# A hybrid encoder layer in split float32: the high halves of streamed weight chunks are asked for one chunk further ahead than the low halves

## The chip, the cores and the metric

The kernel runs on one core of a Trainium2 chip. The metric is device time in microseconds (us), the median of several runs. The kernel before takes 702.0 us, the median of 3 runs (702.0, 702.2, 700.14).

## The reference

One layer, sequence 512, model width 1024, one batch, everything float32. `h` is the RMS-normed input, and its projection `z = h @ w_in` feeds two groups of heads; then an output projection, a SwiGLU block and a gated embedding follow:

```
h = rms_norm(x, g_mix); z = h @ w_in
c_q, c_kv, k_r, hq, hf_f, hf_b, hi, hg = split(z)
a = mla(c_q, c_kv, k_r, ...)         # 4 heads of latent attention, dense softmax
r = hgrn2(hq, hf_f, hf_b, hi, hg, ...)   # 4 heads, gated linear recurrence, both directions
x = x + concat(a, r) @ w_o
h = rms_norm(x, g_ffn); x = x + (silu(h @ w_gate) * (h @ w_up)) @ w_down
gate = sigmoid(rms_norm(x, g_ple) @ w_ple_gate); x = x + gate * (p @ w_ple_proj)
```

The part up to and including `w_o` is called the mixer here, the SwiGLU block the FFN.

## The kernel before

Activations lie transposed, model width on the 128 partitions and the 512 tokens along a row. Each float32 operand of a large product is split into a rounded high part and a low remainder, and a product is three matmuls (`mm3`, lines 141 to 144): high by high (L142), low by high (L143), high by low (L144). Transposes, the recurrence and the sums of squares use plain float32 matmuls.

The mixer streams its weights in 30 chunks of 128x1024 floats (512 KB): 12 for the recurrence's queries and forget gates (`w_hf`), 4 for its values (`w_i`), 4 for its output gates, 4 for the attention's half of `w_o` (`w_oa`), 2 for `w_pp`, 4 for the other half of `w_o` (`w_or`). A chunk has a high tile (`whi`) and a low tile (`wlo`). `weights` (line 148) fills them. The first two chunks are loaded by SyncE as raw float32 and split by ScalarE and VectorE. For the other 28, GpSimd's queue starts a DMA that casts while it loads, which gives the high part (L155); ScalarE writes its negative into the low tile (L156); and a second GpSimd DMA of the same 512 KB adds the source to it (L157), which leaves the remainder. So each chunk is read twice, and its second read waits for a ScalarE copy, which waits for the first.

`wnext` hands out the chunks in order and keeps `AHEAD = 3` of them requested. `wpool` has 4 buffers of each kind (`WB`), 3 of the raw kind, so the high tile of a chunk goes where that of the chunk 4 before it was, once TensorE is done with that.

All other tiles of 128x512 come from a queue of slots of 2 KB a partition: `SLOTS = 74` slots, given out first in, first out. When the mixer ends, `wpool` is closed, and 22 slots (`SLOTS2`) in its place join the queue; the FFN takes its weights (`halves`, L1024, and `pair_seven`, L1102), its sums and its activations from it, so the number of slots says how far its loads can run ahead.

TensorE's work in the mixer is two streams merged: the dense one (products of the streamed chunks, tiles `wi`, `wt`, `wo`, `pp`) and the latency-bound one (attention and recurrence: tiles `s` scores, `p` softmax, `pT` transposed softmax, `av` values, `pd`, `px`, `pk`, `po`). The latency stream has 5 PSUM banks, given out in turn: a bank that held scores `s` becomes free when ScalarE has made `p` of them (L557). The order on each engine is then set by a scheduler, which plays a timeline while the kernel is built; so an edit of one request moves instructions on all engines.

Of the kernel before, what the change touches and what calls it, by code (L numbers as in the profile page):

```python
# [9 lines left out]
F32R = mybir.dt.float32r  # L10
# [5 lines left out]
P = 128  # L16
# [4 lines left out]
EPS = 1e-6  # L21
QK_SCALE = 192 ** -0.5
FPARTS = (4, 4, 4, 4, 3, 3)
SLOTS = 74
SLOTS2 = 22
DAHEAD = 2

# [1 line left out]
AHEAD = 3  # L29
WB = 4  # L30
# [4 lines left out]
LO_DVE = 2  # L35
# [82 lines left out]
def layer_kernel(ctx: ExitStack, tc: tile.TileContext, io, out):  # L118
    nc = tc.nc
    act, dve, pool, pe, sp = nc.scalar, nc.vector, nc.gpsimd, nc.tensor, nc.sync  # L120
# [6 lines left out]
    wpool = mixer.enter_context(tc.tile_pool(name="wpool", bufs=WB))  # L127
    A = Slots(spool, SLOTS, "u")
    B = Slots(ppool, 8, "b")


    def split(hi, lo, src, scale=None, eng=dve):

        if scale is None:
            act.activation(hi, src, AF.Copy)  # L135
            eng.tensor_tensor(lo, src, hi, ALU.subtract)  # L136
        else:
            act.activation(hi, src, AF.Copy, scale=scale)
            dve.scalar_tensor_tensor(lo, src, scale, hi, ALU.mult, ALU.subtract)
# [5 lines left out]

    nw = [0]

    def weights(src, cols, by_dma=False):


        nw[0] += 1
        hi = wpool.tile([P, 1024], F32R, tag="whi", name=f"whi{nw[0]}")
        lo = wpool.tile([P, 1024], F32R, tag="wlo", name=f"wlo{nw[0]}")
        if by_dma:
            pool.dma_start(hi[:, :cols], src)  # L155
            act.activation(lo[:, :cols], hi[:, :cols].bitcast(F32), AF.Copy, scale=-1.0)  # L156
            pool.dma_start(lo[:, :cols], src, accum_op=ALU.add)  # L157
        else:
            raw = wpool.tile([P, 1024], F32, tag="raw", bufs=RAWB, name=f"raw{nw[0]}")
            sp.dma_start(raw[:, :cols], src)  # L160
            split(hi[:, :cols], lo[:, :cols], raw[:, :cols])
        return hi, lo
# [126 lines left out]
    def load_k(k):  # L289

        if k:
            sp.dma_start(xT[k], io["xT"][k])
        raw = wpool.tile([P, 1024], F32, tag="raw", bufs=RAWB, name=f"rawl{k}")
        hi = wpool.tile([P, 1024], F32R, tag="whi", name=f"whil{k}")
        lo = wpool.tile([P, 1024], F32R, tag="wlo", name=f"wlol{k}")
        sp.dma_start(raw[:, :256], io["w_q"][:, k * 256 : k * 256 + 256])
        if k == 0:
            sp.dma_start(vec, io["vec"])
        if k == 1:
            sp.dma_start(pos, io["pos"])  # L300
            sp.dma_start(cst[:, C_FREQ:], io["cst"][:, C_FREQ:])
        sp.dma_start(raw[:, 256:576], io["w_kv"][:, k * 320 : k * 320 + 320])
        for c in (slice(0, 256), slice(256, 576)) if k == 0 else (slice(0, 576),):
            split(hi[:, c], lo[:, c], raw[:, c])
            if c.start == 0:
                split(hT[k][0], hT[k][1], xT[k], vec[:, V_MIX + k : V_MIX + k + 1])
        ws.append((hi, lo))
# [10 lines left out]
    for k in range(KT):  # L318
        load_k(k)
        query_k(k)  # L320
        if k == 1:
            rotary_tables()
        squares(sq, xT[k], k == 0)
        if k < KT - 2:
            key_k(k)
# [271 lines left out]

    wlist = deque()
    ahead = deque()
    nd = [0]  # L600

    def wnext():
        while wlist and len(ahead) < AHEAD:
            nd[0] += 1
            ahead.append(weights(*wlist.popleft(), by_dma=nd[0] > LO_DVE))
        return ahead.popleft()

    def w_in_tile(d):

        w = wnext()  # L610
        o = BD.get("wi")
        for k in range(KT):
            mm3(o, cut(w, k * P, k * P + P), hT[k], k == 0, k == KT - 1)
            if k % 2:
                yield 1.3
        z = A.get("z")
        dve.tensor_tensor(z, o, bc1, ALU.mult)
        BD.put(o)
        d.append(z)

    def w_in_tokens(evacuate):

        for half in range(2):
            ws = [wnext(), wnext()]
            for jp in range(2):
                o = [BD.get("wt0"), BD.get("wt1")]
                for c in range(2):
                    for k in range(4 * c, 4 * c + 4):
                        a = (k % 4) * 256
                        for i in range(2):  # L630
                            j = 2 * jp + i
                            mm3(o[i][:, :256], cut(hT[k], j * P, j * P + P), cut(ws[c], a, a + 256), k == 0, k == KT - 1)
                        if k % 2:
                            yield 1.3
                for i in range(2):
                    evacuate(2 * jp + i, slice(half * 256, half * 256 + 256), o[i][:, :256])
                BD.put(*o)
# [242 lines left out]
    def w_o_half(half, src, banks):  # L880

        for c in range(2):
            ws = [wnext() for _ in range(2)] if half else None
            os_ = []
            for m in range(4 * c, 4 * c + 4):
                if not half and m % 2 == 0:
                    w = wnext()
                o = banks.get("wo")
                os_.append(o)
                if half:  # L890
                    continue
                for k in range(4):
                    a = ((m % 2) * 4 + k) * P
                    mm3(o, cut(w, a, a + P), src[k], k == 0, k == 3)
                dve.tensor_tensor(xT[m], xT[m], o, ALU.add)
                banks.put(o)
                yield 2.6
            if half:

                ki = [(k, i) for k in range(4) for i in range(4)]  # L900
                for k, i in ki if c == 0 else sorted(ki, key=lambda x: x[1]):
                    a = ((i % 2) * 4 + k) * P
                    mm3(os_[i], cut(ws[i // 2], a, a + P), src[k], k == 0, k == 3)
                for i in range(4):
                    residual(4 * c + i, os_[i], V_FFN, sq2, h2)
                banks.put(*os_)
# [283 lines left out]
    f = 0  # L1190
# [136 lines left out]
```

## Time and profile before

| what | value |
|---|---|
| median of 3 runs | 702.0 us |
| the profiled execution | 700.41 us |
| its span on the core | 698.6 us |
| TensorE (matmul) busy | 686.4 us, 98% |
| VectorE busy | 509.5 us, 73% |
| ScalarE busy | 383.2 us, 55% |
| GpSimd busy | 111.1 us, 16% |
| read from HBM | 88.33 MB, 129 GB/s over the span |

The profiled execution took 700.41 us, of which the span on the core is 698.6 us; the remaining 1.8 us lie around it. TensorE was at its full granted clock all the way. Engines are PE (TensorE), PEld (its weight loads), DVE (VectorE), ACT (ScalarE), POOL (GpSimd), SP (SyncE); a q behind a name means its sequencer. An arrow `<-` behind an idle time names what ended it.

### The profile page before, as it was taken

Reading aid. Unit: us, or ns where it says so; the run is one execution under the profiler, and the core shown is the slowest. Engines: PE = TensorE matmul, PEld = TensorE weight load, DVE = VectorE, ACT = ScalarE, POOL = GpSimd, SP = SyncE. Lnnn points to the kernel's source line nnn. Section 1 sums busy time; section 2 is a strip of 40 time slices with the busy share of each in tenths; the row PEclk is TensorE's granted clock in tenths of the full one; section 3 lists DMA queues with packets and bytes.
Section 4 is the critical chain, followed back from the end, with each engine's and each line's share of the span. In section 5 each row is a group of like instructions: output and inputs, shape, how many; then the busy total and the mean of one; then the engine's idle time right before and its main releaser. Section 6 shows DMA issues by size and latency. Waiting matters only on the chain.

```text
span 698.6 us, 11350 instructions
## 1 busy us (share of the span) xinstructions
PE 686.4 (98%) x4170; PEld 604.2 (86%) x4170; DVE 509.5 (73%) x1031; ACT 383.2 (55%) x808; POOL 111.1 (16%) x144
## 2 busy tenths in 40 slices
PE   9999999899999999999989999999999999999997
PEld 8888887699878888878788999999999999998886
DVE  6944489797987943679987977877677578768663
ACT  7857795686645645535544554445544545546421
POOL 6233421101212222010111100001100110100000
PEclk9999999999999999999999999999999999999999
DMA  7575555543657657322456456345655664563111
GB/s 241 164 171 136 124 145 97 119 86 84 157 123 208 156 138 189 90 66 61 147 129 163 115 145 178 92 115 145 166 130 130 158 138 123 123 179 112 55 60 61
DMA packets 44264, 91.18 MB, mean 131 GB/s; under 512 B 5424, under 2 KB 11568, under 8 KB 44208
## 3 DMA queue, kind: packets, MB, share of 16 engines
q0 software_dynamic: 14976, 41.43, 28.8%
q1 hardware_dynamic: 29232, 49.02, 22.3%
q8 instruction: 33, 0.54, 0.3%
q14 instruction: 23, 0.19, 0.1%
HBM read 88.33 MB, written 2.10 MB: 129 GB/s over the span
## 4 chain that ended last, share of the span: by engine, by line
PE 86%; issue 8%; DMA 2%; ACT 2%; POOL 1%; DVE 1%; SPq 0%; POOLq 0%; ACTq 0%
PE p L144 8%; PE p L143 8%; PE p L142 8%; PE dn L143 5%; PE dn L144 5%; PE dn L142 5%; PE wi L143 4%; PE wi L142 4%; PE wi L144 4%; PE pg L144 2%; PE pg L142 2%; PE pg L143 2%; PE wo L142 2%; PE wo L144 2%; PE wo L143 2%
## 5 line engine op out<-in xcount | busy, mean ns | idle before, releaser
L142 PE MATMUL p<-bh,whi 128*128 128x256 f32 x432 | 122.3, 284 | 2.4 <-ACT whi L135 2.3
L143 PE MATMUL p<-bl,whi 128*128 128x256 f32 x432 | 121.8, 283 | 0.0
L144 PE MATMUL p<-bh,wlo 128*128 128x256 f32 x432 | 121.3, 283 | 0.0
L142 PEld LDWEIGHTS p<-bh,whi 128*128 128x128 f32 x432 | 82.7, 192 | 3.3 <-ACT whi L135 3.2
L143 PEld LDWEIGHTS p<-bl,whi 128*128 128x128 f32 x432 | 82.8, 192 | 0.1
L144 PEld LDWEIGHTS p<-bh,wlo 128*128 128x128 f32 x432 | 82.5, 192 | 0.1
L143 PE MATMUL dn<-al,whi 128*128 128x512 f32 x176 | 68.7, 390 | 0.0
L144 PE MATMUL dn<-ah,wlo 128*128 128x512 f32 x176 | 68.5, 389 | 0.0
L142 PE MATMUL dn<-ah,whi 128*128 128x512 f32 x176 | 67.7, 390 | 0.0
L1170 POOL DMA_DIRECT2D wlo<-in_w_d x32 | 27.4, 877 | 202.4 <-ACT wlo L1169 160.5
L1112 DVE TENSOR_TENSOR S<-A,A 128x512 f32<-128x512 f32 x36 | 24.4, 689 | 40.0 <-DMA A<-in_w_up 19.5
L135 ACT ACTIVATE whi<-A 128x512 fp32r<-128x512 f32 x54 | 33.6, 626 | 35.0 <-DMA A<-in_w_gate 22.8
L142 PE MATMUL wi<-hh,whi 128*128 128x512 f32 x128 | 51.2, 400 | 0.0
L144 PE MATMUL wi<-hh,wlo 128*128 128x512 f32 x128 | 50.9, 397 | 0.0
L143 PE MATMUL wi<-hl,whi 128*128 128x512 f32 x128 | 50.5, 394 | 0.0
L135 ACT ACTIVATE whi<-S 128x512 fp32r<-128x512 f32 x72 | 42.6, 623 | 10.3 <-DVE S L1112 9.0
L156 ACT ACTIVATE wlo<-whi 128x1024 fp32r<-128x1024 f32 x28 | 29.7, 1060 | 33.4 <-DMA whi<-in_w_hf 12.0
L136 DVE TENSOR_TENSOR wlo<-S,whi 128x512 fp32r<-128x512 f32 x72 | 46.3, 681 | 1.0 <-ACT whi L135 1.0
L135 ACT ACTIVATE whi<-raw 128x512 fp32r<-128x512 f32 (+2 forms) x42 | 25.5, 625 | 31.6 <-DMA raw<-in_w_up 9.7
L136 DVE TENSOR_TENSOR wlo<-A,whi 128x512 fp32r<-128x512 f32 x54 | 36.8, 682 | 3.1 <-ACT whi L135 3.1
L144 PEld LDWEIGHTS dn<-ah,wlo 128*128 128x128 f32 x176 | 33.1, 188 | 6.9
L142 PEld LDWEIGHTS dn<-ah,whi 128*128 128x128 f32 x176 | 33.0, 188 | 6.4
(342 smaller groups left out, 1840.6 us busy)
## 6 DMA issues: line engine op xcount, KB each, us to landing
A<-in_w_gate SPq DMA_DIRECT2D x36, 256.0 KB, 4.4
A<-in_w_up SPq DMA_DIRECT2D x36, 256.0 KB, 3.8
wlo<-in_w_d POOLq DMA_DIRECT2D x32, 256.0 KB, 5.3
whi<-in_w_hf POOLq DMA_DIRECT2D x14, 512.0 KB, 4.6
wlo<-in_w_hf POOLq DMA_DIRECT2D x14, 512.0 KB, 5.7
raw<-in_w_d SPq DMA_DIRECT2D x24, 256.0 KB, 2.8
x<-in_xT SPq DMA_DIRECT2D x16, 256.0 KB, 4.4
raw<-in_w_pg SPq DMA_DIRECT2D x16, 256.0 KB, 3.5
```

Of the source, the lines that this page charges most:

```text
L135: act.activation(hi, src, AF.Copy)
L136: eng.tensor_tensor(lo, src, hi, ALU.subtract)
L142: pe.matmul(o, lhsT=l[0], rhs=r[0], start=start, stop=False)
L143: pe.matmul(o, lhsT=l[0], rhs=r[1], start=False, stop=False)
L144: pe.matmul(o, lhsT=l[1], rhs=r[0], start=False, stop=stop)
L156: act.activation(lo[:, :cols], hi[:, :cols].bitcast(F32), AF.Copy, scale=-1.0)
L1112: dve.tensor_tensor(r[n], r[a], r[b], op)
L1170: pool.dma_start(lo[:, n], src, accum_op=ALU.add)
```

## The change

`weights` is cut in two. `high` takes a high tile and starts its casting DMA; `weights` gets that tile and does the rest (ScalarE's copy and the adding DMA). `wnext` asks for the high part of one chunk more before it asks for the low part of the oldest chunk that has none. High tiles get 5 buffers, which is 4 KB a partition more, and `SLOTS` falls from 74 to 72, which is 4 KB less.

```diff
-SLOTS = 74
+SLOTS = 72
...
-    def weights(src, cols, by_dma=False):
+    def high(src, cols):
...
+        hi = wpool.tile([P, 1024], F32R, tag="whi", bufs=WB + 1, name=f"whi{nw[0]}")
+        pool.dma_start(hi[:, :cols], src)
+        return hi
+
+    def weights(src, cols, hi=None):
...
+        by_dma = hi is not None
+        if not by_dma:
+            nw[0] += 1
+            hi = wpool.tile([P, 1024], F32R, tag="whi", bufs=WB + 1, name=f"whi{nw[0]}")
         lo = wpool.tile([P, 1024], F32R, tag="wlo", name=f"wlo{nw[0]}")
         if by_dma:
-            pool.dma_start(hi[:, :cols], src)
             act.activation(lo[:, :cols], hi[:, :cols].bitcast(F32), AF.Copy, scale=-1.0)
             pool.dma_start(lo[:, :cols], src, accum_op=ALU.add)
...
     def wnext():
-        while wlist and len(ahead) < AHEAD:
+        while wlist and len(ahead) + len(highs) <= AHEAD:
+            c = wlist.popleft()
             nd[0] += 1
-            ahead.append(weights(*wlist.popleft(), by_dma=nd[0] > LO_DVE))
+            highs.append((*c, high(*c)) if nd[0] > LO_DVE else c)
+            if len(highs) > 1 or nd[0] <= LO_DVE:
+                ahead.append(weights(*highs.popleft()))
+        if len(ahead) < AHEAD and highs:
+            ahead.append(weights(*highs.popleft()))
         return ahead.popleft()
```

Line numbers behind the first function shift by 8, behind `wnext` by 15. The numbers at the ends of tile names also shift by a few.

On GpSimd's queue, around the value chunks (`in_w_i`), the order before is high part, low part of the same chunk, high part of the next:

```order
L155 DMA whi_1511<-in_w_i 128x1024
L157 DMA wlo_1512<-in_w_i 128x1024
L155 DMA whi_1624<-in_w_i 128x1024
L157 DMA wlo_1625<-in_w_i 128x1024
L155 DMA whi_1705<-in_w_i 128x1024
```

In the changed kernel the low part of a chunk stands behind the high part of the next one (`wlo_1515` belongs to `whi_1436`, `wlo_1628` to `whi_1513`):

```order
L152 DMA whi_1513<-in_w_i 128x1024
L165 DMA wlo_1515<-in_w_i 128x1024
L152 DMA whi_1626<-in_w_i 128x1024
L165 DMA wlo_1628<-in_w_i 128x1024
L152 DMA whi_1707<-in_w_i 128x1024
```

Each high part has moved up by one low part on this queue; the number of DMAs is the same.

On ScalarE, during the softmax of the second attention head, the order before has the copy of chunk 14 (`wlo_1625`) directly ahead of the last exponential, `p_1404`:

```order
L557 ACTIVATE p_1364,mx<-s_1356,mx 128x512
L557 ACTIVATE p_1384,mx<-s_1376,mx 128x512
L156 ACTIVATE wlo_1625<-whi_1624 128x1024
L557 ACTIVATE p_1404,mx<-s_1396,mx 128x512
L135 ACTIVATE pTh_1423<-pT_1418 128x512
```

In the changed kernel that chunk's copy (`wlo_1628` of `whi_1513`) stands four exponentials earlier, and the copy near `p_1406` is that of the next chunk and behind it:

```order
L164 ACTIVATE wlo_1628<-whi_1513 128x1024
L565 ACTIVATE p_1318,mx<-s_1310,mx 128x512
L565 ACTIVATE p_1337,mx<-s_1329,mx 128x512
L700 ACTIVATE z_795<-z_795 128x512
L700 ACTIVATE t_1468<-t_1468 128x512
L565 ACTIVATE p_1366,mx<-s_1358,mx 128x512
L565 ACTIVATE p_1386,mx<-s_1378,mx 128x512
L135 ACTIVATE pTh_1425<-pT_1420 128x512
L751 ACTIVATE dm<-dm 128x24 x2
L565 ACTIVATE p_1406,mx<-s_1398,mx 128x512
L164 ACTIVATE wlo_1709<-whi_1626 128x1024
```

The copies have moved from ahead of the softmax they stood in to places further from it.

On SyncE's queue, at the start of the FFN's second part, the order before asks for the last plain weights (`raw`) and then for the four blocks of the first pair of `pair_seven` (`A_507` to `A_510`):

```order
L1024 DMA raw_3709<-in_w_gate 128x512
L1024 DMA raw_3742<-in_w_up 128x512
L1024 DMA raw_3748<-in_w_up 128x512
L1102 DMA A_507_3811<-in_w_gate 128x512
L1102 DMA A_509_3815<-in_w_up 128x512
L1102 DMA A_508_3813<-in_w_up 128x512
L1102 DMA A_538_3997<-in_w_gate 128x512
L1102 DMA A_510_3817<-in_w_gate 128x512
```

The changed kernel asks for them in a similar order, out of 72 + 22 slots:

```order
L1039 DMA raw_3703<-in_w_gate 128x512
L1039 DMA raw_3709<-in_w_gate 128x512
L1117 DMA A_509_3815<-in_w_up 128x512
L1039 DMA raw_3742<-in_w_up 128x512
L1117 DMA A_510_3817<-in_w_gate 128x512
L1117 DMA A_507_3811<-in_w_gate 128x512
L1117 DMA A_508_3813<-in_w_up 128x512
L1117 DMA A_538_3997<-in_w_gate 128x512
```

The same loads stand there; `A_509` has moved ahead of the last plain weight.

## Rows read from the trace of the kernel before

**Rows 1.** The page, share of the span by engine: busy us (share), number of instructions.
```profile
PE 686.4 (98%) x4170; PEld 604.2 (86%) x4170; DVE 509.5 (73%) x1031; ACT 383.2 (55%) x808; POOL 111.1 (16%) x144
```

**Rows 2.** Busy us by stretch: length, then each engine (instructions), clock, DMA share, GB/s.
```profile
100.00:120.00 20.00, 20.00 (x92) 16.50 (x91) 18.94 (x50) 14.15 (x29) 4.30 (x5) 1.00 0.48 106
120.00:140.00 20.00, 17.48 (x90) 13.17 (x89) 15.34 (x39) 11.55 (x24) 3.68 (x5) 1.00 0.53 113
...
340.00:360.00 20.00, 17.36 (x108) 14.72 (x109) 18.21 (x33) 11.24 (x21) 3.38 (x5) 1.00 0.60 159
```

**Rows 3.** Timeline of PE, 124 to 130 us: start, duration, instruction [idle before <- releaser].
```profile
126.42 0.39 PE L144 MATMUL wi<-hh,wlo 128*128 128x512 f32 x1
126.66 0.39 PE L142 MATMUL wi<-hh,whi 128*128 128x512 f32 x1
129.40 0.55 PE L571 MATMUL pT<-cst,p 128*128 128x128 f32 x3 [2.35 <-ACT p L557]
```

**Rows 4.** Timeline of ACT, 122 to 130 us.
```profile
124.99 0.19 ACT L557 ACTIVATION_READ_ACCUMULATOR p<-s,mx 128x1 f32 x1
127.62 1.06 ACT L156 ACTIVATE wlo<-whi 128x1024 fp32r<-128x1024 f32 x1 [2.44 <-issue]
128.58 0.67 ACT L557 ACTIVATE p<-s,mx 128x512 f32<-128x512 f32 x1
```

**Rows 5.** Timeline of POOL, 108 to 132 us.
```profile
110.58 0.55 POOL L155 DMA_DIRECT2D whi<-in_w_i  x1 [2.22 <-PE wi L144]
119.74 0.85 POOL L157 DMA_DIRECT2D wlo<-in_w_i  x1 [8.61 <-ACT wlo L156]
120.29 1.13 POOL L155 DMA_DIRECT2D whi<-in_w_i  x1
```

**Rows 6.** DMA issues of 118 to 131 us, KB each, us from issue to landing.
```profile
wlo<-in_w_i POOLq DMA_DIRECT2D x2, 512.0 KB, 5.4
whi<-in_w_i POOLq DMA_DIRECT2D x1, 512.0 KB, 7.3
```

**Rows 7.** DMA issues of 0 to 118 us.
```profile
whi<-in_w_i POOLq DMA_DIRECT2D x1, 512.0 KB, 3.9
```

**Rows 8.** Waits of 0 to 345 us, ScalarE's copies L156: us in total, times, longest.
```profile
ACT wlo L156 <- DMA whi<-in_w_hf: 12.0, 7, 6.8
...
ACT wlo L156 <- DMA whi<-in_w_oa: 7.8, 3, 3.6
...
ACT wlo L156 <- DMA whi<-in_w_pp: 3.8, 1, 3.8
...
ACT wlo L156 <- DMA whi<-in_w_or: 3.7, 3, 2.4
```

**Rows 9.** Timeline of PE, 122 to 131 us: a step from wi to transposes and back.
```profile
123.73 0.40 PE L144 MATMUL wi<-hh,wlo 128*128 128x512 f32 x1
123.97 0.63 PE L571 MATMUL pT<-cst,p 128*128 128x128 f32 x4
124.35 0.48 PE L142 MATMUL wi<-hh,whi 128*128 128x512 f32 x1
124.67 0.40 PE L143 MATMUL wi<-hl,whi 128*128 128x512 f32 x1
```

**Rows 10.** First use of the value chunks by PE, of the rows of tile wlo.
```profile
L143 PE MATMUL wt<-wlo,hh x64: 277/283/365, 141.4 to 184.0; 128*128 128x256 f32 x64
```

**Rows 11.** Timeline of PE, 336 to 358 us.
```profile
350.04 0.39 PE L142 MATMUL p<-bh,whi 128*128 128x256 f32 x1 [1.11 <-ACT whi L135]
...
355.45 0.39 PE L142 MATMUL p<-bh,whi 128*128 128x256 f32 x1 [1.24 <-ACT whi L135]
```

**Rows 12.** Busy us by stretch, as rows 2, of 345 to 355 us.
```profile
345.00:350.00 5.00, 3.93 (x18) 2.82 (x17) 4.12 (x7) 3.06 (x6) 1.91 (x3) 1.00 0.84 244
350.00:355.00 5.00, 4.14 (x28) 3.52 (x28) 4.09 (x8) 1.78 (x4) 0.37 (x1) 1.00 0.99 242
```

**Rows 13.** SyncE's queue, 285 to 360 us: what its loads waited for.
```profile
SPq L1024 <- DVE t L1079: 14.1, 1, 14.1
SPq L1024 <- PE wo L144: 10.9, 2, 10.7
SPq L1024 <- PE ff L143: 10.8, 1, 10.8
```

**Rows 14.** DMA issues of 340 to 356 us.
```profile
A<-in_w_up SPq DMA_DIRECT2D x4, 256.0 KB, 4.8
```

More of the change, by code (lines that the diff above doesn't have):

```diff
@@ L146, in layer_kernel @@
     nw = [0]
-    def weights(src, cols, by_dma=False):
+    def high(src, cols):
         nw[0] += 1
-        hi = wpool.tile([P, 1024], F32R, tag="whi", name=f"whi{nw[0]}")
+        hi = wpool.tile([P, 1024], F32R, tag="whi", bufs=WB + 1, name=f"whi{nw[0]}")
[6 more added lines that the diff above has]
+            hi = wpool.tile([P, 1024], F32R, tag="whi", bufs=WB + 1, name=f"whi{nw[0]}")
         lo = wpool.tile([P, 1024], F32R, tag="wlo", name=f"wlo{nw[0]}")
         if by_dma:
-            pool.dma_start(hi[:, :cols], src)
             act.activation(lo[:, :cols], hi[:, :cols].bitcast(F32), AF.Copy, scale=-1.0)
@@ L293, in load_k @@
         raw = wpool.tile([P, 1024], F32, tag="raw", bufs=RAWB, name=f"rawl{k}")
-        hi = wpool.tile([P, 1024], F32R, tag="whi", name=f"whil{k}")
+        hi = wpool.tile([P, 1024], F32R, tag="whi", bufs=WB + 1, name=f"whil{k}")
         lo = wpool.tile([P, 1024], F32R, tag="wlo", name=f"wlol{k}")
@@ L599, in layer_kernel @@
     ahead = deque()
+    highs = deque()
     nd = [0]
     def wnext():
-        while wlist and len(ahead) < AHEAD:
+        while wlist and len(ahead) + len(highs) <= AHEAD:
+            c = wlist.popleft()
             nd[0] += 1
-            ahead.append(weights(*wlist.popleft(), by_dma=nd[0] > LO_DVE))
+            highs.append((*c, high(*c)) if nd[0] > LO_DVE else c)
[3 more added lines that the diff above has]
+            ahead.append(weights(*highs.popleft()))
         return ahead.popleft()
```

## The prediction

> **What bounds the kernel now.** I read the page's busy shares first: TensorE is busy 686.4 of 698.6 us, 98%, the next engine 73% [rows 1]. So whatever the change does to other engines counts only where TensorE stands still, and all its idle time is 12.2 us, start and end included. The second view is the busy time in stretches of 20 us. Two stretches inside the kernel fall visibly short: 120 to 140 us, with 17.48 us busy, and 340 to 360 us, with 17.36; the stretch before the first is full [rows 2]. The first lies in the mixer, where the change works, the second in the first part of the FFN, where only the two slots it takes away reach. The granted clock is 1.00 in both, so these are waits.
>
> The third view is the timeline of 120 to 131 us on three engines, to be read backwards. TensorE starts a `wi` matmul at 126.66 and the next instruction, a transpose `pT`, at 129.40; it waited 2.35 us for ScalarE's exponential `p` [rows 3]. At the ordinary step of 0.24 us (126.42 to 126.66, same rows) the hole costs 2.74 - 0.24 = 2.5 us. All four inputs of that transpose had served earlier transposes, so what it waits for must be the PSUM bank that the late exponential still reads. ScalarE had finished the exponential before it at about 125.2, then stood still for 2.44 us, made the low-part copy L156 of a weight chunk at 127.62, and only then the exponential, at 128.58 [rows 4]. Its queue runs in order, so the exponential waited behind the copy, and the copy for its chunk's high part. The profile names the releaser "issue"; the DMA view shows the cause: that high part took 7.3 us from issue to landing [rows 6], and 120.29 + 7.3 = 127.6 is when the copy starts. GpSimd had issued it 0.55 us after the adding DMA of the chunk ahead [rows 5]; an earlier one of the same size, `in_w_i` in an uncrowded stretch, landed after 3.9 us [rows 7]. So the mixer's one hole is a high part asked for too late and behind another transfer.
>
> **The change, part by part.** *Requests moved.* 28 casting and 28 adding DMAs stay 28 and 28, ScalarE keeps its 28 copies, TensorE its matmuls. Each high part is issued ahead of the low part of the chunk before. Its buffer is that of the chunk five before, so the request does not wait longer than the low part it now precedes, which waits for the chunk four before its own, the same chunk. GpSimd is blocked no more than before: it waits for what it would have waited for one instruction later.
>
> *The hole at 126.66.* The copy of that chunk now stands four exponentials earlier on ScalarE, its data asked for a whole chunk earlier; the copy near the critical exponential stands behind it. I take the whole 2.5 us off, less 0.1 for what any reordering leaves: **-2.4 us**. Bounds: 0 if another wait takes the place, -2.5 at most.
>
> *ScalarE's other waits for high parts.* 12.0 + 7.8 + 3.8 + 3.7 = 27.3 us [rows 8]. TensorE's two stretches show that, apart from the one hole, they were hidden behind dense matmuls; I cost their going at 0. The cover is the dense stream, and it stays.
>
> *Order of TensorE.* Written out, the old order changes 137 times between plain float32 products (transposes, recurrence) and split ones, the new one 121 times: 8 visits fewer. A visit costs a little: the matmul after four transposes takes 0.32 us to the next (124.35 to 124.67) against 0.24 otherwise [rows 9], so some 0.1 us with its entry. 8 x 0.1 = **-0.8 us**; bounds 0 and -1.5.
>
> *The low parts.* Each now stands behind a high part on the same software queue. From the rows, following another transfer cost 7.3 - 3.9 = 3.4 us [rows 6, 7]. Cover: the low part of the first value chunk was issued at 119.74 and landed 5.4 us later, at 125.1 [rows 5, 6]; its first use is at 141.4 [rows 10], 16 us on. I cost it at 0. The Trainium skill ("DMA: Bandwidth & Descriptors", section "Queues, rings and completion order") says that each DMA engine consumes descriptors in ring order; it speaks against this change, as it makes every low part the later of two. The trace agrees with it in the one pair above, 7.3 us for the follower; by it the sum is the same as long as the 16 us stand.
>
> *Two slots fewer, 94 instead of 96 in the FFN.* There loads do wait for slots: 14.1, 10.9 and 10.8 us in single waits [rows 13]. When slots come free, the transfers bunch: a DMA share of 0.84 and 0.99 in 345 to 355 us [rows 12], and TensorE waits 1.11 and 1.24 us for splits of these weights [rows 11]. No row shows the price of a slot. From below: 0, if the slots in question are free anyway. From above: a slot carries a 256 KB load that takes 4.8 us there [rows 14], so two loads that each fall in line behind a released slot add at most 2 x 4.8 = 9.6 us. SyncE's order is nearly the old one, so I take 0, nearest to the end at which the same events release the same loads, and keep the upper end for the range.
>
> *The start.* One high part is now issued ahead of the first `rs_tok` on GpSimd; such an issue takes 0.55 to 1.13 us [rows 5], and TensorE has dense work of several us there: 0.
>
> **Sum.** -2.4 - 0.8 = -3.2 us against the profiled execution's 700.4: 697.2 us. That execution lies 1.6 us below the median of the runs shown (702.0), and half of that, 0.8, is added for a median: **698.0 us**. A measurement of this kernel can tell about 0.3%, 2.1 us, from no change; -3.2 is just beyond it.
>
> **The rivals.**
>
> *A new hole for the old one (no change).* All engines' orders are drawn anew by the scheduler. ScalarE's copies, which used to come when their data had landed, now tend to wait for the low buffer, that is for TensorE to finish the chunk four before. If a copy stands ahead of an exponential or of a `kT` of the recurrence and TensorE still has one piece of that chunk ahead of it, say 12 matmuls of 0.24 us, 2.9 us, it costs about what the old hole did. For it: ScalarE's queue is in order, and the old hole was of this kind. Against it: one such hole in the 28 copies before. Time: 698.0 + 2.9 = 700.9 us.
>
> *The FFN starved by two slots (slower).* The stage of 340 to 360 us is the one place where TensorE waits for loads. If one load falls in line, +4.8; if both do, +9.6, against -3.2 elsewhere. Midway, 698.0 + 7.2 = 705.2 us. It decides from 3.2 + 2.1 = 5.3 us of added waiting in that stretch. For it: the DMA share of 0.99 and the long slot waits. Against it: one in 48 slots is little, and the long waits are for events (sums of blocks, finished products) that a slot more or less does not move.
>
> *The low parts come late (no change).* If followers land 3.4 us late, the rule of the ring order would show as TensorE waiting at a chunk's first high-by-low matmul (L144). Once it would cost 3.4 us: 698.0 + 3.4 = 701.4. The cover of 16 us speaks against it, the 7.3 us of the one follower for it. The page named above has the rule that gives it.
>
> *The change does not do what it says.* Excluded by the order: each high part does stand one low part earlier on GpSimd's queue.
>
> **How the numbers follow.** Forecast, the hole gone and nothing of size new: 0.50. New hole: 0.25. Late low parts: 0.05. FFN starved: 0.20. Within the forecast case a gain of 3.2 with its bounds of 0 to 4 us falls short of 2.1 about one time in seven, 0.07; the starved FFN ends slower by over 0.3% in 0.15 and within in 0.05; the new hole goes faster in 0.05, slower in 0.03, same in the rest. Faster 0.50 - 0.07 + 0.05 = 0.48; slower 0.15 + 0.03 = 0.18; same 0.34. The range: the forecast's own is 698.0 less 2 (a smaller FFN wait, since some FFN splits now come before the mixer's end) and plus 1.5; the no-change cases reach to 701.4; what lies above is most of the starved case. 695.5 to 703.0 leaves out 0.15 above and about 0.05 below.
>
> **What would show it.** Right: TensorE idle for `p` L557 under 0.5 us in 120 to 140; ScalarE's waits of L156 for high parts down from 27.3 us to under 8; adding DMAs landing later than 5.4 us after their issue, with no wait of TensorE at L144 in the mixer; the stretch of 340 to 360 us near its 17.4 us busy; everything after it earlier by about 3 us. Wrong: a hole of over 2 us at another place in 30 to 300 us, then the first rival; a busy time under 14 us in 340 to 360, then the second; waits at L144 for a DMA of `wlo`, then the third. A span within 1 us of 698.6 with the hole gone would mean that the gain was given back in the FFN, and the sum lacked that term.

## The result and the profile after

The changed kernel takes **693.7 us** (median; 693.2 to 694.6), the kernel before 701.7 us beside it: a ratio of 0.9873, interval 0.984 to 0.9906. The gain is 8.0 us, and 693.7 lies below the range that the forecast gave. Of the two profiled executions, the one after takes 693.5 us with a span of 691.7, against 700.4 and 698.6: 6.9 us are to be found in the traces.

The page after, the line that answers to [rows 1]: TensorE has lost 3.8 us of busy time and 3.1 us of idle time, ScalarE is 3.3 us busier.

```profile
PE 682.6 (99%) x4170; PEld 604.6 (87%) x4170; DVE 510.3 (74%) x1031; ACT 386.5 (56%) x808; POOL 108.7 (16%) x144
```

Busy time by stretch, after (columns as in [rows 2]). Both stretches that fell short before are full, 17.48 and 17.36 us then, 20.00 now. In exchange TensorE falls short in 320 to 340 us, 18.27 us busy against 19.86 before, while VectorE (the third engine of the row) has no hole there in either kernel:

```profile
120.00:140.00 20.00, 20.00 (x113) 16.81 (x112) 17.42 (x48) 13.63 (x28) 2.04 (x4) 1.00 0.49 101
...
320.00:340.00 20.00, 18.27 (x78) 13.82 (x77) 20.00 (x41) 10.29 (x18) 0.00 (x0) 1.00 0.17 52
340.00:360.00 20.00, 20.00 (x146) 18.89 (x145) 18.98 (x33) 12.34 (x24) 3.44 (x5) 1.00 0.66 187
```

TensorE's waits after (total, times, longest). The transpose that waited 2.35 us for the exponential [rows 3] is not among them, and a product has to wait for a late low part, once:

```profile
PE wo L142 <- ACT ppo L967: 0.9, 1, 0.9
PE ff L142 <- ACT whi L135: 0.9, 1, 0.9
PE wi L144 <- DMA wlo<-in_w_hf: 0.7, 1, 0.7
PE dn L142 <- ACT ah L135: 0.5, 1, 0.5
```

ScalarE's copies (now L164) waited 27.3 us for high parts [rows 8]; they wait 3.4 us for them now, and else for TensorE to give back a low buffer:

```profile
ACT wlo L164 <- PE wi L144: 5.7, 5, 2.2
ACT wlo L164 <- PE wt L143: 4.0, 3, 2.6
ACT wlo L164 <- DMA whi<-in_w_hf: 3.4, 1, 3.4
```

And the requests of 118 to 131 us (KB each, us to landing), 7.3 and 5.4 us before [rows 6]:

```profile
whi<-in_w_i POOLq DMA_DIRECT2D x2, 512.0 KB, 3.8
wlo<-in_w_i POOLq DMA_DIRECT2D x2, 512.0 KB, 6.1
```

**Where the time went.** Three places in the two timelines cut the span: the first residual sum of the output projection's last half (VectorE), the first FFN product `ff`, and the last product `p` (TensorE). Two more lines stand with them: the end of the last head (`rTl`) and the first step of the block sums (`xa`), both on VectorE. Before:

```profile
286.72 0.69 DVE L136 TENSOR_TENSOR rTl<-r,rTh 128x512 fp32r<-128x512 f32 x1 [3.14 <-ACT rTh L135]
...
289.95 2.48 DVE L999 TENSOR_TENSOR x<-x,wo 128x512 f32<-128x512 f32 x4 [1.09 <-PE wo L144]
...
295.19 0.39 PE L142 MATMUL ff<-hh,whi 128*128 128x512 f32 x1
...
316.61 0.74 DVE L1077 SCALAR_TENSOR_TENSOR xa<-x,vec,rsbc 128x512 f32<-128x512 f32 x1
...
625.79 0.28 PE L144 MATMUL p<-bh,wlo 128*128 128x256 f32 x1
```

After:

```profile
276.31 0.68 DVE L136 TENSOR_TENSOR rTl<-r,rTh 128x512 fp32r<-128x512 f32 x1
...
281.19 2.48 DVE L1014 TENSOR_TENSOR x<-x,wo 128x512 f32<-128x512 f32 x4 [4.20 <-PE wo L144]
...
291.87 0.39 PE L142 MATMUL ff<-hh,whi 128*128 128x512 f32 x1
...
311.43 0.74 DVE L1092 SCALAR_TENSOR_TENSOR xa<-x,vec,rsbc 128x512 f32<-128x512 f32 x1
...
618.91 0.28 PE L144 MATMUL p<-bh,wlo 128*128 128x256 f32 x1
```

By the first `ff` the changed kernel is 3.3 us ahead, about what the forecast summed. From the first `ff` to the last `p`, a stage whose code the change does not touch, it takes 327.0 us instead of 330.6 and gains 3.6 more. Everything behind keeps its length. Of the 3.6 us, 1.8 are waits of TensorE, 3.5 us in the stage before and 1.7 after; the other 1.8 are steps between products that are 0.1 to 0.2 us longer than usual, of which the kernel before has more, mostly in the first 20 us of the stage and around 345 to 355 us. I call that stretch the **FFN stage**, and the time from the first residual sum to the first `ff` the **lead** of the residuals: 5.2 us before, 10.7 after.

### The profile page after: what moved, and what is told of

It reads as the page before. It is cut to its first block, busy times and chain, and to the rows that moved or that the text cites. A ratio compares the mean times of both kernels' runs of the same rounds, so it can differ in the third digit from the quotient of the medians.

```text
span 691.7 us, 11366 instructions
## 1 busy us (share of the span) xinstructions
PE 682.6 (99%) x4170; PEld 604.6 (87%) x4170; DVE 510.3 (74%) x1031; ACT 386.5 (56%) x808; POOL 108.7 (16%) x144
## 4 chain that ended last, share of the span: by engine, by line
PE 88%; DVE 5%; DMA 4%; issue 1%; ACT 1%; SPq 1%; ACTq 0%; DVEq 0%
PE p L144 9%; PE p L143 9%; PE p L142 9%; PE dn L143 6%; PE dn L144 6%; PE dn L142 6%; PE wi L144 4%; PE wi L143 4%; PE wi L142 4%; PE pg L144 2%; PE pg L143 2%; PE pg L142 2%; PE wo L144 2%; PE wo L142 2%; PE wo L143 2%; PE po L852 1%
## 5 line engine op out<-in xcount | busy, mean ns | idle before, releaser
L144 PE MATMUL p<-bh,wlo 128*128 128x256 f32 x432 | 122.2, 283 | 0.0
L144 PEld LDWEIGHTS p<-bh,wlo 128*128 128x128 f32 x432 | 82.9, 192 | 0.2 <-DVE wlo L136 0.2
L144 PE MATMUL dn<-ah,wlo 128*128 128x512 f32 x176 | 68.5, 389 | 0.0
L144 PE MATMUL wi<-hh,wlo 128*128 128x512 f32 x128 | 50.6, 395 | 0.7 <-DMA wlo<-in_w_hf 0.7
L144 PEld LDWEIGHTS dn<-ah,wlo 128*128 128x128 f32 x176 | 33.0, 188 | 7.0
L136 DVE TENSOR_TENSOR wlo<-raw,whi 128x512 fp32r<-128x512 f32 (+2 forms) x42 | 28.5, 687 | 14.5 <-ACT whi L135 14.3
L164 ACT ACTIVATE wlo<-whi 128x1024 fp32r<-128x1024 f32 x28 | 29.8, 1063 | 16.2 <-PE wi L144 5.7
```

The source lines that it names most:

```text
L144: pe.matmul(o, lhsT=l[1], rhs=r[0], start=False, stop=stop)
```

## The experiments

One table first; what each run was for follows. Stage and lead are read as above from one profiled execution each; the mixer is the time from the first `wi` product to the first `ff`; times are medians, with the interval of the ratio to the kernel before. One execution is a rough measure. Two of one order (the kernel before and e4_ahead4) differ by 0.8 us in the stage and 0.3 in the mixer. Six kernels (the changed one, e2_slots2_24, e5_slots2_20, x1_hold, r1_after, r2_after) share TensorE's order from the first `wi` for 228 us; that stretch took from 227.8 to 229.8 us, mostly because a low part near 41 us came 0 to 1.4 us late. And some stages hold a time at the lower clock (last section): it took 3.4 us each from x3_six, x1_hold, e1_slots72 and y1_l96, 1.7 from x2_l104 and another 1.7 from its mixer. The whole time of the kernel before lay between 697.8 and 706.2 us in 25 executions of one session.

| kernel | high buffers | slots in the FFN | mixer us | lead us | FFN stage us | time us (ratio) |
|---|---|---|---|---|---|---|
| before | 4 | 96 | 263.1 | 5.2 | 330.6 | 701.7 |
| e4_ahead4 | 4 | 96 | 263.4 | 5.2 | 329.9 | 700.6 (0.9952 to 1.0001) |
| x5_raw2 | 5 | 96 | 258.7 | 7.5 | 328.3 | 696.2 (0.9904 to 0.9947) |
| e2_slots2_24 | 5 | 96 | 257.4 | 10.2 | 328.4 | 694.2 (0.983 to 0.9903) |
| x2_l104 | 4 | 96 | 267.5 | 10.9 | 328.2 | 703.3 (1.0002 to 1.0034) |
| x3_six | 6 | 94 | 261.7 | 3.0 | 338.1 | 707.8 (1.0065 to 1.0116) |
| x1_hold | 5 | 94 | 259.2 | 4.6 | 335.6 | 700.5 (0.9949 to 0.9997) |
| e1_slots72 | 4 | 94 | 261.7 | 5.5 | 335.6 | 704.7 (1.0017 to 1.0063) |
| y1_l96 | 5 | 94 | 257.0 | 6.1 | 334.0 | 697.3 (0.9909 to 0.9955) |
| y2_l101 | 5 | 94 | 260.5 | 7.6 | 329.1 | 697.4 (0.9912 to 0.9959) |
| after | 5 | 94 | 259.9 | 10.7 | 327.0 | 693.7 (0.984 to 0.9906) |
| e5_slots2_20 | 5 | 92 | 260.2 | 8.4 | 327.5 | 694.2 (0.9828 to 0.9908) |

### The parts of the change, one at a time

**e1_slots72**, the slots alone, in the kernel before:

```diff
-SLOTS = 74
+SLOTS = 72
```

> The kernel before with 72 small buffers instead of 74 and nothing else (four high buffers as before, so 94 slots in the FFN). The changed kernel gained 8.0 us: 3.3 us by the first FFN matmul (295.19 to 291.87) and 3.5 us between there and the last FFN product (625.79 to 618.91 for both). Theory S (the second gain is the FFN's order, which two slots fewer redraw): 701.7 - 3.5 = 698.2, first ff still near 295.2, and the stalls of TensorE of 1.3 and 1.4 us at 348.6 and 353.9 gone. Theory M (the second gain comes from the end of the mixer, whose last residuals start 8.7 us earlier with the fifth buffer): 701.7 here, the two stalls stay. Both: the stall of 2.5 us at 126.7 stays, since only the fifth buffer can take it away.

Measured: 704.7 us, slower; stage 335.6. Theory S has fallen in its plain form: with a short lead the order that two slots fewer draw costs 5.0 us here, 3.4 of them by the clock. And the last sentence was wrong too: the stretch from 120 to 140 us is full (20.00 us of TensorE), so a redrawn order can take the old hole away without any buffer, though ScalarE still waits 24.3 us for high parts.

**e2_slots2_24**, the slots given back, in the changed kernel:

```diff
-SLOTS2 = 22
+SLOTS2 = 24
```

> The changed kernel with the two slots given back to the FFN (72 in the mixer, 96 in the FFN as before). Its TensorE order is the changed kernel's in the mixer and the kernel's before in the first part of the FFN. Theory S: the mixer's gain stays (first ff near 291.9) and the FFN's goes: 693.7 + 3.5 = 697.2, with TensorE stalls of over 2 us together near 345 to 351. Theory M: 693.7, no such stalls. Half and half: 695.4.

Measured: 694.2 us, no different from the changed kernel's 693.7. The stage takes 328.4 us, with nearly the kernel before's order of TensorE in its first part; there it took 330.6. So most of the FFN's gain, 2.2 of 3.6 us, came without the two slots (1.5 us against e4_ahead4's execution); theory M stands. The two stalls of [rows 11] shrink to 0.6 and 0.4 us here and do not go. So the lead alone, 10.2 us here, does not remove them; the 94 slots of the changed kernel also draw another order at that place.

**e4_ahead4**, the request's place alone (against the changed kernel):

```diff
-SLOTS = 72
+SLOTS = 74
...
-        hi = wpool.tile([P, 1024], F32R, tag="whi", bufs=WB + 1, name=f"whi{nw[0]}")
+        hi = wpool.tile([P, 1024], F32R, tag="whi", name=f"whi{nw[0]}")
```

> The changed program's request of the high part one chunk ahead, with four high buffers and 74 slots. The order of instructions on all five engines is that of the kernel before, instruction by instruction: the scheduler had put each request as early as a buffer was free already, wherever the program's text had it. Expected by every theory of the buffers and slots: 701.7, same within 0.3%. A theory by which the request's place in the text matters for itself: 701.7 - 3.3 = 698.4.

Measured: 700.6 us, the same. The counterpart, the fifth buffer and 72 slots without the queue of high parts in the text, has the changed kernel's order on all five engines, instruction by instruction (it was not run for its time). So what the section on the change puts down to the request's place in the text is the work of the fifth buffer: the scheduler puts each request as early as a buffer is free.

**e5_slots2_20**, the changed kernel with 92 slots:

```diff
-SLOTS2 = 22
+SLOTS2 = 20
```

> The changed kernel with 92 slots in the FFN instead of 94 (72 in the mixer). Theory S in its form that fewer slots help as such (later requests, less clash of transfers): below 693.7, to about 692. In its form that the order is redrawn by chance with every size: anything between 690 and 700, the difference to 693.7 arising between 291.9 and 360 us alone. Theory M: 693.7. A loss by starvation, as the forecast's rival had it: above 697, with SyncE's waits for slots.

Measured: 694.2 us, stage 327.5. No starvation and no further gain: theory M's number.

### Is it the lead?

**x1_hold**: the changed kernel with its last products held back on TensorE (`held` has the weights and banks of both groups of four tiles).

```diff
+                # products k < 3 of all eight tiles, the last one is e
+                with tc.issue_after(e.ins):
+                    for i in range(4):
+                        one(*held[0], 3, i)
+                for i in range(4):
+                    residual(i, held[0][1][i], V_FFN, sq2, h2)
```

> The changed kernel with the last products of the output projection's second half held back: the k=3 products of its first four tiles are issued behind the second four's k=2 products, so that all eight residuals come in a bunch as in the kernel before. Up to that place the order of all engines is the changed kernel's. The FFN stage (first ff matmul to last p matmul) took 330.6 us before, 327.0 in the changed kernel; the first residual add came 5.2 us ahead of the first ff matmul before, 10.7 in the changed kernel (10.2, 8.4 and 5.5 in the kernels with 96 slots, 92 slots, and four high buffers with 94 slots, whose FFN stage took 328.4, 327.5 and 335.6). Theory L (the FFN's gain is this lead of the residuals, which the last head's earlier end allows): lead down to about 5, FFN stage back to 329.5 to 331, time 696 to 697.5; the mixer's gain stays (first ff near 291.9). Theory O (the FFN's gain comes from the order of its own TensorE work or from the buffers): 693.7, FFN stage near 327.

Measured: the first `ff` comes at 291.43, so the mixer keeps its gain; the lead is 4.6 us, the stage 335.6, the time 700.5. Theory L is right in kind and too small in size: the stage loses 8.5 us, not 3. Waits make 4.0 of them and the lower clock 3.4. The edit does more than take back the lead: it also holds the last products of eight tiles in one bunch. The residuals, their low parts and the seven sums of squares now queue on VectorE. TensorE's waits, with two of a length that the changed kernel has nowhere in the stage, on a low part of VectorE's and on the sum of squares:

```profile
PE ff L144 <- DVE wlo L136: 1.6, 1, 1.6
PE ss L192 <- DVE sq L218: 1.4, 1, 1.4
```

**x2_l104**, a long lead in the kernel before, by one weight of the planner:

```diff
-L_TOTAL, D_TOTAL = 97, 135
+L_TOTAL, D_TOTAL = 104, 135
```

> The kernel before (four high buffers, 74 slots, high parts as before) with one weight of the planner changed, 97 to 104 for the stream of the heads, so that the last head ends earlier in the order: 82 matmuls of the output projection lie behind its last transpose, where the kernel before has 55 and the changed one 79. Theory L: the first residual leads the first ff matmul by 9 us or more, the FFN stage falls from 330.6 to about 327 to 328.5, whatever the mixer does; if the mixer keeps its time, 698.5. Theory O: FFN stage stays near 330.6. The mixer may gain or lose some us by the redrawn order, which no theory here prices; read the stage, not the sum.

Measured: lead 10.9, stage 328.2, as theory L had it, with four buffers and the old slots. The mixer lost 4.4 us to new stalls (one `pT` waits 4.2 us) and the clock, so the time is 703.3.

**x3_six**, a sixth buffer (against the changed kernel):

```diff
-SLOTS = 72
-SLOTS2 = 22
+SLOTS = 70
+SLOTS2 = 24
...
-tag="whi", bufs=WB + 1
+tag="whi", bufs=WB + 2
```

> The changed kernel with a sixth high buffer, paid with two more small buffers (70 in the mixer, 94 in the FFN). Its order has only 42 output projection matmuls behind the last head's last transpose. Theory L: the lead of the residuals falls to 4 us or below and the FFN stage takes 330 or more, although there is one more buffer; with a mixer like the changed kernel's, 697 or more. A theory by which the fifth buffer's gain is a matter of enough buffers: 693.7 or below. Waits of ScalarE for high parts of under 6 us in all by either.

Measured: 707.8 us, ScalarE without any wait for a high part, lead 3.0 and stage 338.1, the worst of all. More buffers are not more gain.

**x5_raw2**, five buffers and all the slots (against the changed kernel):

```diff
-SLOTS = 72
-RAWB = 3
+SLOTS = 74
+RAWB = 2
```

> Five high buffers with all 74 slots (96 in the FFN), paid instead with one of the three buffers for raw weights, which only the first ten chunks use. It parts the buffer from the slots in the mixer. The buffer's own effect on the mixer, as the forecast had it (the 2.5 us stall of TensorE at 126.7 gone, fewer waits of ScalarE for high parts): first ff near 292 unless the start is later. Its order has 65 output projection matmuls behind the last transpose, between before (55) and changed (79). Theory L: a lead of 7 to 8 us and an FFN stage of 328 to 329.5; time about 695.5. If the slots made the mixer's gain: first ff near 295.

Measured: the first `wi` comes 2.8 us later than before (34.8), for lack of the raw buffer, and the first `ff` yet 1.7 us earlier (293.5): the mixer itself gains 4.4 us, where the slots alone gained 1.4. The first is more than the 2.0 us by which executions of one order differ, the second is not: the mixer's gain is mostly the buffer's. Lead 7.5, stage 328.3, time 696.2, near the 695.5 of theory L.

**y1_l96** and **y2_l101**, the changed kernel with that one weight at 96 and at 101:

```diff
-L_TOTAL, D_TOTAL = 97, 135
+L_TOTAL, D_TOTAL = 96, 135
```

```diff
-L_TOTAL, D_TOTAL = 97, 135
+L_TOTAL, D_TOTAL = 101, 135
```

> The changed kernel with the planner's weight of the heads' stream at 96 instead of 97 and nothing else: five high buffers, the same slots. Its order has 59 output projection matmuls behind the last head's last transpose instead of 79, so the residuals lead the first ff matmul by about 5.5 us. Theory L: FFN stage 334 to 336 as in the two other kernels with 94 slots and a lead of about 5 (335.6 both), time near 701 with a mixer like the changed kernel's. If the fifth buffer or the 94 slots gave the FFN's gain: FFN stage near 327.

> The changed kernel with that weight at 101: the order in the mixer is redrawn, but 79 matmuls lie behind the last transpose, as in the changed kernel. Theory L: lead of 10 us or more and FFN stage 326.5 to 328, whatever the mixer takes. If the FFN's time hangs on chance in the redrawn order: anything from 327 to 336.

Measured for 96: lead 6.1, stage 334.0, as theory L has it, while the mixer happens to take 2.9 us less than the changed kernel's, so that the time is 697.3. Its waits on the residuals' chain are those of x1_hold:

```profile
PE ff L144 <- DVE wlo L136: 1.8, 2, 1.6
PE ss L192 <- DVE sq L218: 1.3, 1, 1.3
```

For 101 the lead came out at 7.6, not 10: the number of products behind the last transpose does not fix it. The stage, 329.1, lies between those of 6.1 and 10.7. So with 94 slots six kernels line up: leads of 3.0, 4.6, 5.5, 6.1, 7.6 and 10.7 us, stages of 338.1, 335.6, 335.6, 334.0, 329.1 and 327.0. Less the clock's 3.4 us, the first four are 334.7, 332.2, 332.2 and 330.6, and the row still falls. With 96 slots it levels off: leads of 5.2, 7.5, 10.2 and 10.9 us go with 330.6 (329.9 in e4_ahead4), 328.3, 328.4 and 328.2.

### Why a lead is worth time

In the kernel before, VectorE is busy without a hole when the block sums come:

```profile
320.00:340.00 20.00, 19.86 (x88) 16.13 (x88) 20.00 (x42) 10.79 (x20) 0.00 (x0) 1.00 0.21 53
```

Four runs took subtractions from it there. The edit (f >= 1; **r2_after** has f >= 2):

```diff
+            if by_dma:
+                hi, lo = A.get("whi", F32R), A.get("wlo", F32R)
+                c = slice(i * 512, i * 512 + 512)
+                pool.dma_start(hi, src[:, c])
+                act.activation(lo, hi.bitcast(F32), AF.Copy, scale=-1.0)
+                pool.dma_start(lo, src[:, c], accum_op=ALU.add)
+                ws.append((hi, lo))
+                continue
...
-            w = halves(io[name][f])
+            w = halves(io[name][f], f >= 1)
```

> The kernel before with 0.69 us VectorE subtractions taken away from the FFN's first part: for f = 1, 2, 3 the low parts of w_gate and w_up come by an adding DMA (12 subtractions, 8.3 us), and the high parts by a casting DMA. The residuals still come late (lead near 5.2 us). Theory V (the lead is worth something because VectorE is the limit there: it was busy without a hole from 315 to 345 us): FFN stage from 330.6 to 327 to 328.5, TensorE's stalls after 340 us under 1 us, time 698.5 to 700. Theory T (the lead helps by ScalarE's or the sum of squares' chain, not by VectorE's load): FFN stage near 330, time 701 to 702. A loss by the DMA's added traffic and GpSimd's issues: above 702.

> The same relief of VectorE in the kernel with the residuals held back (lead 4.6 us, FFN stage 335.6, time 700.5). Theory V: the FFN stage falls by 3 us or more, to 332.5 or less, since the 1.6 us stall on a low part that VectorE makes (ff) and those after it go, time 697.5 or less. The 1.4 us stall on the sum of squares ahead of it stays by both, being of the residuals themselves. Theory T: FFN stage 334 to 336.

> The same relief in the changed kernel (lead 10.7 us, FFN stage 327.0, TensorE's stalls in it 1.7 us in all). Theory V: what is left to gain is small, 0.5 to 1.7 us: 692 to 693.2. Theory T: 693.7. A loss is possible by the order that is redrawn, up to 1.5 us.

> As the run before it, for f = 2, 3 alone (8 subtractions, 5.5 us). Theory V: between the changed kernel and the run with 12, 692.3 to 693.7. Theory T: 693.7.

Measured: the stage fell from 330.6 to 327.8 in the kernel before, and from 335.6 to 329.1 in x1_hold, the lead nearly or quite unchanged (5.5 and 4.6 us). That is what theory V gave for the stage, and T did not. The proof is not clean. In x1_hold with relief 3.4 of the 6.4 us are the clock, which did not fall inside the stage, and the wait for the sum of squares, which was to stay by both theories, is gone. And the edit spares the FFN 12 `raw` slots as well as 12 subtractions; no run parts the two. Slots alone, with a lead of 8 us or more, hardly moved the stage (328.4, 327.0 and 327.5 us with 96, 94 and 92). Where the expectations failed is outside of that place. The new requests on GpSimd's queue make low parts late, in x1_hold ahead of the first `ff`:

```profile
PE wo L144 <- DMA wlo<-in_w_or: 3.0, 1, 3.0
```

and in the changed kernel, whose lead was long enough anyway, inside the stage, which went from 327.0 to 332.0:

```profile
PE ff L143 <- DVE hl L139: 2.1, 3, 0.9
PE ff L144 <- DMA wlo<-in_w_gate: 1.9, 1, 1.9
```

The first of these two waits is the old hole's kind again. ScalarE's copy for a new low part stood 5.2 us waiting for its high part, with the residuals' high parts behind it in the queue, and VectorE waited 6.6 us for those:

```profile
288.97 0.75 DVE L139 SCALAR_TENSOR_TENSOR hl<-x,vec,hh 128x512 fp32r<-128x512 f32 x1 [6.63 <-ACT hh L138]
```

The times: 700.1 (0.9955 to 1.0005) for the kernel before with relief, 699.7 (0.9935 to 0.998) for x1_hold, 697.6 (0.9914 to 0.9968) for the changed kernel, a loss of 4. With 8 subtractions, r2_after, 692.0 us (0.981 to 0.9888): the lowest median of the study, but its interval covers most of the changed kernel's, and its stage (328.3 us, 1.7 of them by the clock) is no shorter. It is not shown to beat it.

## Why the prediction was wrong, step by step

**The hole at 126.66: right.** The wait is gone and the copy no longer stands in front of the exponential. The net term is smaller than the -2.4 us: waits of 0.7 and 0.9 us, at a late low part and at the evacuation of `pp`, came in its place (the first is chance, 0 to 1.4 us among executions of this order), so that TensorE's waits between the first `wi` and the first `ff` fell from 2.5 to 1.6 us.

**The order of TensorE: right in sign, too small.** The rest of the mixer, without waits, went from 260.6 to 258.3 us, -2.3 where the forecast had -0.8. Counted from the first `wi` to the first `ff`, the changes between plain and split products fall from 160 to 144, 16 fewer, as the forecast had counted. That these 16 changes cost the 2.3 us is argued, not shown: y2_l101 has 138 of them and a rest of 259.6 us, x2_l104 142 and 261.3, of which 1.7 are the clock's. The two terms together gave -3.2 for the mixer, as measured: luck, by errors that cancel, and within the 2.0 us by which executions of one order differ.

**ScalarE's waits, the low parts, the start: right for the mixer.** Waits for high parts fell from 27.3 to 3.4 us at no visible price; adding DMAs land after 6.1 us instead of 5.4, and one of 28 made TensorE wait, 0.7 us. Standing behind a high part costs the low parts no more than that here. The first `wi` is at 31.96, 0.1 us earlier.

**Two slots fewer, costed at 0 with a loss alone as its bound: this step failed.** It took the FFN's stalls at 350 and 355 us [rows 11] for a matter of slots and loads, because the DMA share was 0.99 there [rows 12], and so priced the FFN by its slots only. The runs show that the stage depends on when VectorE can begin: the last head ended its chain (`rTl`) at 276.3 us instead of 286.7, the residuals began 8.8 us earlier against 3.3 for TensorE, and the block sums at 311.4 instead of 316.6. VectorE's full stretch then ends at 340.96 us, before TensorE's first of the seven products at 343.83 (before: 345.54 and 339.83), and the two stalls are gone. That is not the lead's work alone: TensorE now comes to that product 7 us later behind its first `ff`, and with a like lead and nearly the old order (e2_slots2_24) the stalls stay at 0.6 and 0.4 us. x1_hold, which takes the lead back and bunches the last products, has stalls and more than the lost time again. The sum had no term for a chain that runs off the critical path through the mixer and comes onto it behind. This missing term measured -2.2 us with 96 slots (e2_slots2_24) and -3.6 with 94; the 1.3 us between the two are little more than two executions of one order differ by. How much of it is VectorE's load itself is not shown cleanly (see the relief runs). What of the 10.4 us of the last head's earlier end is ScalarE's freed queue, whose waits the forecast costed at 0, and what is the redrawn order stays open: with the slots alone it ended at 283.1, with the buffer alone at 282.3.

**The rivals.** The FFN starved by two slots was priced at 705.2 us; e1_slots72, the two slots with a short lead, takes 704.7. The nearness is luck, for the mechanism is another: in the FFN stage TensorE waits 2.4 us for the sum of squares and 1.6 for a split on VectorE, which is busy without a hole there, and the lower clock takes 3.4 us. The new hole and the late low parts came in small, as told. That the request's place in the text does not do what it says was excluded too quickly: the order had moved, but by the buffer (e4_ahead4).

**What was to show it.** Of five signs two came true whole (no hole, waits under 8 us) and one by half: adding DMAs land later, but TensorE did wait once at L144 in the mixer, 0.7 us. The stretch of 340 to 360 us was to stay near 17.4 us busy and everything behind to be 3 us earlier; 20.00 and 6.9 told of the missing term.

**The size.** 3.2 us of the mixer and 3.6 of the FFN give the 6.9 of the traces. The medians differ by 8.0, since the profiled execution before lies 1.3 us under its median and the one after at its own.

## What to carry to other kernels

A chain that is hidden in one stage can be what the next stage begins with. When a change frees an in-order queue, follow also what ends earlier without being waited for, up to the stage where a second engine is full, and give that a term with both signs. Where a scheduler draws the order, an edit of two slots or of one planner weight moved this kernel by 3 to 4 us; a gain should be put down to a mechanism only when undoing that mechanism alone takes it back, and a price be read only against the spread of executions of one order.

## What the runs showed of the hardware

The stages with a short lead lose more than their waits, because TensorE's clock falls. In e1_slots72 TensorE waits 2.4 us for the sum of squares and then runs one-column products; the timeline of TensorE shows the steps of `ff` behind it at 0.42 to 0.43 us, and at 0.23 again six us later:

```profile
308.38 1.58 PE L184 MATMUL ss<-ones,sq 128*128 128x1 f32 x8 [2.36 <-DVE sq L210]
...
311.25 0.63 PE L142 MATMUL ff<-hh,whi 128*128 128x512 f32 x1
311.67 0.63 PE L143 MATMUL ff<-hl,whi 128*128 128x512 f32 x1
...
316.00 0.39 PE L142 MATMUL ff<-hh,whi 128*128 128x512 f32 x1
316.23 0.39 PE L143 MATMUL ff<-hl,whi 128*128 128x512 f32 x1
```

The granted clock (the figure ahead of the DMA share) is 0.50 there, the 1.2 GHz level:

```profile
306.00:308.00 2.00, 0.01 (x1) 0.00 (x0) 1.66 (x3) 0.79 (x2) 0.00 (x0) 1.00 0.00 0
308.00:310.00 2.00, 1.62 (x9) 1.63 (x10) 0.33 (x2) 0.00 (x0) 0.00 (x0) 0.68 0.00 0
310.00:312.00 2.00, 2.00 (x5) 1.61 (x6) 0.85 (x5) 0.00 (x0) 1.03 (x1) 0.50 0.00 0
312.00:314.00 2.00, 2.00 (x6) 1.52 (x6) 1.23 (x5) 0.00 (x0) 0.00 (x0) 0.50 0.00 0
314.00:316.00 2.00, 2.00 (x7) 1.53 (x6) 0.00 (x0) 0.00 (x0) 0.00 (x0) 0.61 0.00 0
316.00:318.00 2.00, 2.00 (x10) 1.68 (x9) 0.00 (x0) 0.00 (x0) 0.00 (x0) 1.00 0.00 0
```

From these rows the fall took 3.4 us of work (0.32, 0.50, 0.50 and 0.39 of 2 us each), less what TensorE idled at 308, more than the wait itself. x1_hold, y1_l96 and x3_six fell at the same place, behind waits of 1.4, 1.3 and 2.1 us for the sum of squares, and a second time near 355, 351 and 360 us (0.83 over 350 to 360 us in the first two). Each of these falls took 1.7 us of work.

Waits as long elsewhere cost no clock: the hole before, 2.35 us [rows 3], and one of 2.7 us in e5_slots2_20, in this stretch, both at 1.00:

```profile
320.00:340.00 20.00, 17.11 (x74) 13.38 (x73) 20.00 (x40) 10.50 (x19) 0.00 (x0) 1.00 0.32 100
```

And others did. In r1_before the old hole itself, 2.56 us at the same transposes and with products of the same kind behind it, was followed by a granted clock of 0.50 over 130 to 132 us; in r2_after a wait of 1.8 us at a dense product of the FFN was, with 0.83 over 340 to 350 us:

```profile
129.96 0.90 PE L571 MATMUL pT<-cst,p 128*128 128x128 f32 x3 [2.56 <-ACT p L557]
...
342.69 0.39 PE L142 MATMUL p<-b11h,whi 128*128 128x256 f32 x1 [1.77 <-ACT whi L135]
```

So in these runs neither the length of a wait nor the products behind it tell whether it costs clock. The four waits named in front of the one-column products did; of the others some did and some did not.
